# Writing out pair one of a Strassen-blocked projection by hand, and spreading the row factors with a split diagonal on TensorE

## The chip, the cores and the metric

The kernel runs on one core of one Trainium2 chip. The metric is the device time of one execution in microseconds; lower is better. All arithmetic is float32 in and out; the matrix products run on TensorE in its fp32r type, each operand split into a high and a low part and multiplied in three passes (high times low, low times high, high times high).

The engines are named as in the profile: PE is TensorE's matmul, PEld its weight load, DVE is VectorE, ACT is ScalarE, POOL is GpSimd and SP is SyncE, which issues nearly all transfers. Each engine runs its own instruction queue in order and waits on the others through semaphores.

## The reference, cut to what matters

One layer of a hybrid decoder trunk is applied to 1024 prompt rows and 32 sample rows, 1056 rows of 1024 channels in all. What the change touches is the norm ahead of the projection and the first groups of the projection's 24 column blocks:

```python
def _rmsnorm(x, g):
    xf = x.astype(jnp.float32)
    r = lax.rsqrt(jnp.mean(xf * xf, axis=-1, keepdims=True) + EPS)
    return (xf * r).astype(x.dtype) * g
...
    proj = jnp.einsum('bsd,de->bse', h, w_in)
    b_g, c_g, u, z_a, v, z_b = jnp.split(proj, ...)
    cu = c_g * u                      # then a 3-tap convolution along the rows
    y_a = b_g * yc * jax.nn.silu(z_a)
    # v: mean over a trailing window of 2, 4, 8 or 16 rows, minus the row, a 128x128 map
    y_b = pooled * pool_scale * jax.nn.silu(z_b)
    y = jnp.einsum('bse,ed->bsd', jnp.concatenate([y_a, y_b], axis=-1), w_out)
```

The output rows then get x added and a second norm.

## The kernel before, in words

The rows lie on the free axis: a tile is 128 channels by 1056 rows, cut into three column groups n0, n1, n2 of 352. The kernel does not scale x before the projection. It multiplies the weights by the norm's gain (`gain_w`, line 196), projects the unscaled x, and multiplies the results by the row factor r (`R`, the 1056 factors on every partition) or, for the product of c and u, by its square (`R2`).

The 24 column blocks are taken in twelve pairs (`PAIRS`, line 35). Pair 0 (v and z_b of group 0) is projected plainly while x arrives (`project_first`, line 180); its results stay unscaled in `vb` and `szb_0` (lines 499 and 526). From pair 1 on a pair is two blocks of 128 output channels, done over n0 and n1 by a Strassen scheme with eight block products of 12 matmuls (`block`, line 219), and plainly over n2 (`plain`, `plain1`: 24 matmuls for each side). The names: a block B11, B12, B21, B22 uses the weights as they are (tiles `wa` and `wb`), T1 to T4 use sums of weights (`tw`, made by `make_t`, line 202; split into `wc` and `wd`); S1 to S4 are sums of x made once. The accumulators in PSUM are a, b and c; `s1` is a copy of a after its first block, `t1` and `t2` are b plus `s1` after b's first and second block. `strassen` (line 388) writes one pair: PE order is B11 on a, T2 on b, T1 on c, left plain, B21 on a, T3 on b, right plain, T4 on b, B22 on c. T4 overwrites what `t2` reads, so PE's T4 waits for `t2` (line 439). The three hooks `early`, `middle` and `late` make the next pair's weights: load (1 MB, `load_w`), gain on ACT (8 instructions), sums on DVE, and four splits, each an ACT copy to fp32r (the high part) and a DVE subtraction (the low part), line 151 and 152.

The row factors: rows 0 to 639 are loaded once more row by row (`load_rows`, line 232) and squared on ACT with a sum along the row (`square_rows`, one instruction for each 128 rows, five in all). The other 416 rows are squared from the transposed x (`squares_head`, `squares_last`), summed over channels by DVE (`sums_last`) and over partitions by PE against a column of ones (`sums_rest`, line 265). `rows` (line 273) turns the 128 by 9 table of sums into factors with nine small instructions on DVE and ACT, writes the table to DRAM and reads it back broadcast to all partitions (lines 284 to 286).

What sets the order: inside the block from line 476, the engines PE, ACT, DVE and POOL run in program order, except that a scheduler may interleave this block with what comes after it; in the pairs from 2 on only PE is in program order, and the scheduler places the rest by its own priorities. Buffers are tiles of a pool under a tag; a new tile waits until the old one's readers are done. The tags that matter are `wt` (five buffers for split weights) and `wraw` (one buffer for a pair's raw weights, so that `load_w(p + 1)` waits for the last split of pair p).

Of the kernel before, what the change touches and what calls it, by code (L numbers as in the profile page):

```python
# [62 lines left out]
def trunk(ctx, tc, xt, xres, xct, w_first, w_in, w_out, pool_w, par, fg, sconv, spool,  # L63
# [194 lines left out]
    def sums_last(acc, sq):  # L258
        out = acc[:, REST:TC]
        vt(sq[0], sq[0], sq[1], op=ADD)  # L260
        vt(sq[0][:, :2], sq[0][:, :2], sq[2], op=ADD)
        vt(out, sq[0][:, 0], sq[0][:, 1], op=ADD)
        vt(out, out, sq[0][:, 2], op=ADD)

    def sums_rest(acc):
        pt = bank("rest")
        for t in range(NTT, NTOK):
# [3 lines left out]
            nc.scalar.copy(ss[:m, t:t + 1], pt[:m, i:i + 1])  # L271
# [116 lines left out]
    def strassen(p, S1, S2, S3, S4, hooks):  # L388
# [19 lines left out]
        if p == 1:  # L408
            a, s1, pL, pR = hooks["open"]
        else:  # L410
            a = bank(f"a_{p}")[:, :TN]
            s1 = snap(f"s1_{p}")
            block(a, p, "B11", A11, True, False)
            nc.scalar.copy(s1, a)
# [7 lines left out]
        if p > 1:  # L422
            block(c, p, "T1", S1, True, False)
        if p > 1:
            pL = plain(0, f"l_{p}")
        def scaled(n, pt):
            if p == 1:
                nc.scalar.copy(left[:, n], pt)
            else:
                vt(left[:, n], pt, scale[:, n], op=MUL)  # L430

        scaled(n2, pL)
# [19 lines left out]
        if p > 1:  # L452
            gt(left[:, n1], left[:, n1], scale[:, n1], op=MUL)
# [8 lines left out]
        elif q == "c":  # L462
            gt(up[:, 2:2 + 2 * TN], right[:, both], left[:, both], op=MUL)
# [12 lines left out]
    with tc.manual_schedule(engines={ET.PE, ET.Activation, ET.DVE, ET.Pool}):  # L476
# [38 lines left out]

        S1 = xtile("xa", "S1")
        split(S1, S1f)
        make_unit(1, "c")
        S3 = xtile("xb", "S3")
        split(S3, S3f)  # L520
        S2 = xtile("xc", "S2")
        split(S2, S2f)
        make_unit(1, "d")
        for n in (0, 1):
            for i in range(2):
                nc.scalar.copy(heads[i][:, cols[n]], pm[i, n])
# [4 lines left out]
        pL, pR = plain1(0), plain1(1)  # L531
        a1 = bank("a_1")[:, :TN]
        block(a1, 1, "B11", A11, True, False)
        s1 = snap("s1_1")
        nc.scalar.copy(s1, a1)  # L535
        block(a1, 1, "B21", A12, False, True)

        def early():
            gain_w(2)
            make_t(2)  # L540
            make_unit(2, "a")
            sums_last(acc, sq)

        def middle():
            make_unit(2, "d")
            make_unit(2, "c")
            xk.extend(load_rows(t) for t in range(2, NTT))
            for t in range(NTT):
                square_rows(t, xk[t])
# [256 lines left out]
```

## Time and profile before

| what | value |
|---|---|
| time, median of 3 runs (lowest to highest) | 411.41 us (411.21 to 414.06) |
| the profiled execution: its own time, its span | 411.48 us, 409.7 us |
| PE busy, share of the span | 369.8 us, 90% |
| DVE, ACT, POOL busy | 271.3 us (66%), 174.6 us (43%), 45.5 us (11%) |
| chain that ended last, by engine | PE 70%, DVE 11%, DMA 6%, ACT 6% |
| mean granted TensorE clock | 0.959 |

How to read it: times count from the span's start. A row of a timeline is start, duration, engine, line, operation, out<-in, shapes, and in brackets the idle time before it with what ended it. Two instructions that follow each other on one engine overlap by about 0.1 us in the records, so a row of instructions costs a little less than the sum of their durations; the chain of waits shows the durations without this overlap. A block of 12 matmuls takes 1.94 us there when the granted clock is full.

### The profile page before, as it was taken

How to read it: one execution, taken by the hardware profiler on the slowest of the kernel's cores; microseconds unless marked ns; L12 is line 12 of the kernel's file. 1: busy time of each engine (PE TensorE's matmuls, PEld its weight loads, DVE VectorE, ACT ScalarE, POOL GpSimd, SP SyncE). 2: the span in 40 equal slices, each digit the busy share in tenths (PEclk: the TensorE clock that was granted, in tenths of full speed). 3: DMA queues.
4: the chain of work that ended last, by engine and by line, in shares of the span. 5: the costliest groups of instructions: out<-in, count | busy, mean ns of one | idle time of the engine just before them, and what ended most of it. 6: DMA issues, size and time to landing. Idle time of an engine off the chain costs nothing.

```text
span 409.7 us, 5263 instructions
## 1 busy us (share of the span) xinstructions
PE 369.8 (90%) x2108; PEld 353.3 (86%) x2108; DVE 271.3 (66%) x387; ACT 174.6 (43%) x299; POOL 45.5 (11%) x28
## 2 busy tenths in 40 slices
PE   8999549930699999999999999999999999999993
PEld 5999539930699999999999999999998888999883
DVE  4888486229967878766779675688629926422493
ACT  5894954415252364526163545345107805111211
POOL 0000002005300303200300400020501000000000
PEclk9999887985699999999999999999999999999998
DMA  7932312110050204030020404140646970300042
GB/s 220 417 125 102 104 61 74 46 53 0 0 210 0 104 0 154 3 121 37 18 86 2 155 2 155 29 154 2 200 170 204 379 308 6 150 0 0 2 167 102
DMA packets 14680, 42.23 MB, mean 103 GB/s; under 512 B 4928, under 2 KB 6080, under 8 KB 13248
## 3 DMA queue, kind: packets, MB, share of 16 engines
q1 hardware_dynamic: 14512, 41.57, 28.2%
q8 instruction: 16, 0.26, 0.3%
q10 hardware_dynamic: 144, 0.33, 0.2%
q14 instruction: 8, 0.07, 0.1%
HBM read 33.46 MB, written 8.43 MB: 102 GB/s over the span
## 4 chain that ended last, share of the span: by engine, by line
PE 70%; DVE 11%; DMA 6%; ACT 6%; issue 2%; SPq 2%; POOL 1%; DVEq 0%; POOLq 0%; ACTq 0%
PE b L226 14%; PE po L636 13%; PE a L226 9%; PE pc L706 9%; PE c L226 9%; PE r L226 8%; PE l L226 8%; DMA rows<-mru 3%; DMA raw<-in_xt_dram 3%; DVE win L340 2%; PE pp L362 1%; ACT wraw L200 1%; SPq L106 1%; DMA R<-rows 1%; DVE tw L205 1%
## 5 line engine op out<-in xcount | busy, mean ns | idle before, releaser
L636 PE MATMUL po<-wo,mix 128*128 128x512 f32 (+1 forms) x264 | 56.7, 374 | 0.2 <-DVE mix L152 0.2
L636 PEld LDWEIGHTS po<-wo,mix 128*128 128x128 f32 x264 | 46.2, 188 | 10.2 <-DVE mix L152 0.8
L226 PE MATMUL a<-A,wa 128*128 128x352 f32 x264 | 47.9, 331 | 5.1 <-ACT s L535 5.1
L226 PE MATMUL b<-A,wd 128*128 128x352 f32 x132 | 26.8, 358 | 25.5 <-DVE t L439 25.4
L226 PEld LDWEIGHTS a<-A,wa 128*128 128x128 f32 x264 | 44.7, 194 | 5.4 <-ACT s L535 5.4
L226 PEld LDWEIGHTS b<-A,wd 128*128 128x128 f32 x132 | 24.6, 213 | 26.4 <-DVE t L439 26.4
L200 ACT ACTIVATE wraw<-wraw,gain 128x256 f32<-128x256 f32 x88 | 36.5, 499 | 12.9 <-DMA wraw<-in_w_in_dram 11.4
L226 PE MATMUL l<-pl,wa 128*128 128x352 f32 x240 | 40.4, 324 | 0.0
L226 PE MATMUL r<-pl,wb 128*128 128x352 f32 x240 | 40.4, 324 | 0.0
L226 PEld LDWEIGHTS l<-pl,wa 128*128 128x128 f32 x240 | 39.1, 188 | 0.0
L226 PEld LDWEIGHTS r<-pl,wb 128*128 128x128 f32 x240 | 39.1, 188 | 0.0
L706 PE MATMUL pc<-mix,wo 128*128 128x416 f32 x192 | 36.5, 351 | 0.0
L706 PEld LDWEIGHTS pc<-mix,wo 128*128 128x128 f32 x192 | 35.9, 188 | 0.6
L205 DVE TENSOR_TENSOR tw<-wraw 128x1024 f32<-128x1024 f32 x11 | 13.9, 1265 | 20.1 <-ACT wraw L200 20.1
L226 PE MATMUL b<-S,wc 128*128 128x352 f32 x132 | 23.2, 324 | 0.7 <-DVE t L421 0.7
L226 PE MATMUL c<-S,wb 128*128 128x352 f32 x132 | 23.8, 330 | 0.0
L226 PE MATMUL b<-S,wd 128*128 128x352 f32 x132 | 23.6, 325 | 0.0
L226 PE MATMUL c<-S,wc 128*128 128x352 f32 x132 | 23.4, 324 | 0.0
L151 ACT ACTIVATE wd<-tw 128x1024 fp32r<-128x1024 f32 x11 | 11.6, 1057 | 26.8 <-DVE tw L207 26.8
L226 PEld LDWEIGHTS c<-S,wb 128*128 128x128 f32 x132 | 22.4, 195 | 0.2 <-DVE y L440 0.2
L226 PEld LDWEIGHTS b<-S,wc 128*128 128x128 f32 x132 | 21.6, 188 | 1.0 <-DVE t L421 1.0
L226 PEld LDWEIGHTS b<-S,wd 128*128 128x128 f32 x132 | 21.7, 188 | 0.0
(178 smaller groups left out, 562.5 us busy)
## 6 DMA issues: line engine op xcount, KB each, us to landing
wraw<-in_w_in_dram SPq DMA_DIRECT2D x11, 1024.0 KB, 4.6
woraw<-in_w_out_dram SPq DMA_DIRECT2D x8, 512.0 KB, 6.3
raw<-in_xt_dram SPq DMA_DIRECT2D x4, 704.0 KB, 8.8
zt<-in_xres_dram SPq DMA_DIRECT2D x5, 512.0 KB, 6.7
spill_b<-yb SPq DMA_DIRECT2D x4, 528.0 KB, 4.1
mixraw<-spill_b SPq DMA_DIRECT2D x4, 528.0 KB, 6.8
out_yt_dram<-zt SPq DMA_DIRECT2D x4, 512.0 KB, 2.6
zc<-in_xct_dram SPq DMA_DIRECT2D x4, 416.0 KB, 6.6
```

Of the source, the lines that this page charges most:

```text
L106: nc.sync.dma_start(raw[n][:, k:k + m, :], xt[:, n * KD + k:n * KD + k + m, :])
L151: nc.scalar.activation(hi, src, AF.Copy)
L200: nc.scalar.activation(t, t, AF.Copy, scale=gain[:, k:k + 1])
L205: nc.vector.tensor_tensor(t[:, 0:2], w[:, 2:4], w[:, 0::2], op=ALU.subtract)
L226: nc.tensor.matmul(pt, t[:, a, i, k * P:(k + 1) * P], x[:, b, k], start=first and s == 0, stop=last and s == len(seq) - 1, skip_group_chec ...
L340: nc.vector.tensor_tensor(o[:, lo2:PM + SEQ], a[:, lo2:PM + SEQ], a[:, lo2 - s:PM + SEQ - s], op=ALU.add)
L362: nc.tensor.matmul(pt[:, :TN], pws[:, a, g, :], pooled[g][b][:, cols[n]], start=(s == 0), stop=(s == 2))
L636: nc.tensor.matmul(pt, mix[k][:, b, t * P:(t + 1) * P], wo[k][:, a, c], start=(k == 0 and s == 0), stop=(k == KD - 1 and s == 2))
L706: nc.tensor.matmul(pt, wo[k][:, a, d * P:(d + 1) * P], mix[k][:, b, T0:], start=(k == 0 and s == 0), stop=(k == KD - 1 and s == 2))
```

## The change: the diff, and how it moves instructions

Pair 1 no longer goes through `strassen`; its instructions are written out with the order of each engine, in the block that sets the order of PE, ACT, DVE and POOL. In it DVE makes the weight sums (`make_t(1)`) before the split of `wb`; ACT squares three of the five row tiles early, ahead of the four copies of pair 0's results, and takes the copy `s1` ahead of the two halves of S4; the row tiles lie in `R`, `R2`, `up` and one weight buffer (`x34`, tag `wt`) instead of `R`, `R2` and three tiles of the tag `tmp`. The four sums of `sums_rest` are copied out by two instructions instead of four.

The row factors take another way. `rows` splits the 128 by 9 table into a high part `rh` and a low part and multiplies a 128 by 128 identity (`ident`, made by POOL at the start) with each of the nine columns, which gives two tiles of 128 by 1056 (`dh` on ACT, `dl` on DVE) that are diagonal in each stretch of 128 columns. `rows_out`, called in pair 2 after its T1 block, multiplies them on PE with a 128 by 128 matrix of ones (6 matmuls of 352 columns), and ACT copies the result into `R` (three copies) and squares it into `R2`. The write to DRAM and the broadcast read are gone. What needs `R` (`scale_heads`: `after_u(0)`, `vb`, `szb_0`, `after_v(0)`, the pool weights) moved into pair 2's `early` hook. `pool_linear(0)` comes after pair 3 instead of pair 2, and in the pairs from 2 on POOL is in program order too.

```diff
+    ident = sm.tile([P, 19 * NB], F32, tag="swin", name="ident")[:, :P]
+    nc.gpsimd.memset(ident, 0.0)
+    nc.gpsimd.affine_select(out=ident, in_=ident, compare_op=ALU.not_equal, fill=1.0, base=0,
+                            pattern=[[-1, P]], channel_multiplier=1)
...
         vt(sq[0][:, :2], sq[0][:, :2], sq[2], op=ADD)
+        yield
         vt(out, sq[0][:, 0], sq[0][:, 1], op=ADD)
...
-            nc.scalar.copy(ss[:m, t:t + 1], pt[:m, i:i + 1])
+        nc.scalar.copy(ss[:, NTT:NTOK - 1], pt[:, :NTOK - 1 - NTT])
+        nc.scalar.copy(ss[:NSAMP, NTOK - 1:], pt[:NSAMP, NTOK - 1 - NTT:NTOK - NTT])
...
-        d = tc.dram_tile([NTOK * P], F32, name="rows")
-        nc.sync.dma_start(d.rearrange("(t p) -> p t", p=P), r)
-        nc.sync.dma_start(R, d[:TOK].partition_broadcast(P))
+        rh = sm.tile([P, NTOK], F32R, tag="rh", bufs=1, name="rh")
+        nc.scalar.activation(rh, r, AF.Copy)
+        vt(u, r, rh.bitcast(F32), op=ALU.subtract)
+        dh, dl = (tp.tile([P, TOK], F32R, tag="tmp", name=f"diag_{a}") for a in range(2))
+        for t in range(NTOK):
+            m = min(P, TOK - t * P)
+            nc.scalar.activation(dh[:, t * P:t * P + m], ident[:, :m], AF.Copy, scale=rh[:, t:t + 1].bitcast(F32))
+            nc.vector.tensor_scalar(dl[:, t * P:t * P + m], ident[:, :m], u[:, t:t + 1], None, op0=ALU.mult)
+        return dh, dl
+
+    def rows_out(diag):
+        for n in range(NT):
+            pt = bank(f"pr_{n}")[:, :TN]
+            for a in (1, 0):
+                nc.tensor.matmul(pt, onesr, diag[a][:, cols[n]], start=a == 1, stop=a == 0)
+            nc.scalar.copy(R[:, cols[n]], pt)
         nc.scalar.activation(R2, R, AF.Square)
...
+        block(c, p, "T1", S1, True, False)
+        if p == 2:
+            rows_out(diag)
+            gt(up[:, 2:], up[:, 2:], R2, op=MUL)
+        pL = plain(0, f"l_{p}")
...
-        xk = [load_rows(t) for t in range(2)]
+        xk = [load_rows(t, q[:, :D]) for t, q in enumerate((R, R2, up[:, 2:]))]
...
+        make_t(1)
         make_unit(1, "b")
+        load_w(2)
...
+        x34 = wp.tile([P, 2, D], F32, tag="wt", bufs=5, name="x34")
+        xk += [load_rows(t, x34[:, t - 3]) for t in (3, 4)]
+        for t in range(3):
+            square_rows(t, xk[t])
+        for n in (0, 1):
+            for i in range(2):
+                nc.scalar.copy(heads[i][:, cols[n]], pm[i, n])
+        S2 = xtile("xc", "S2")
+        split(S2, S2f)
+        make_unit(1, "d")
...
+        block(pa, 1, "B11", A11, True, False)
+        nc.scalar.copy(s1, pa)
+        block(pa, 1, "B21", A12, False, True)
         S4 = xtile("xd", "S4")
...
+        sums = sums_last(acc, sq)
+        next(sums)
+        nc.scalar.copy(t_0[:, n2], pL)
+        block(pc, 1, "T1", S1, True, False)
+        block(pb, 1, "T2", S2, True, False)
+        vt(t1, pb, s1, op=ADD)
+        gain_w(2)
+        nc.scalar.copy(t_0[:, n0], pa)
+        make_unit(2, "a")
+        block(pb, 1, "T3", S3, False, False)
+        vt(t2, pb, s1, op=ADD)
+        make_t(2)
+        vt(um[:, n1], pc, t2, op=ADD)
+        for t in (3, 4):
+            square_rows(t, xk[t])
+        make_unit(2, "d")
+        block(pb, 1, "T4", A22, False, True)
+        vt(t_0[:, n1], pb, s1, op=ADD)
+        block(pc, 1, "B22", S4, False, True)
+        vt(um[:, n0], pc, t1, op=ADD)
+        gt(up[:, 2:2 + 2 * TN], um[:, both], t_0[:, both], op=MUL)
+        vt(up[:, 2 + 2 * TN:], pR, t_0[:, n2], op=MUL)
+        for _ in sums:
+            pass
+        make_unit(2, "c")
+        sums_rest(acc)
+        diag = rows()
+        make_unit(2, "b")
...
+    def scale_heads():
+        after_u(0)
+        vt(vb[:, PM:], vb[:, PM:], R, op=MUL)
+        gt(szb[0], szb[0], R, op=MUL)
+        silu(szb[0])
+        pwraw = tmp("pwraw")[:, :NG * P].rearrange("p (g c) -> p g c", c=P)
+        nc.sync.dma_start(pwraw, pool_w)
+        split(pws, pwraw)
+        after_v(0)
...
-        with tc.manual_schedule(engines={ET.PE}):
+        with tc.manual_schedule(engines={ET.PE, ET.Pool}):
             strassen(p, S1, S2, S3, S4, {"early": early, "middle": middle, "late": late})
-            if p == 2:
+            if p == 3:
                 pool_linear(0)
```

Three places show how instructions move. The rows name line, operation, out<-in and size; numbers behind names are buffers.

ACT, in pair 1, up to the copy `s1` (last row). `vb` and `szb` copies are pair 0's results, `S` are the high parts of S3 (raw_88), S2 (raw_89) and S4 (S4f). Before:

```order
L151 ACTIVATE wc_391<-tw_382 128x1024
L151 ACTIVATE S_394<-raw_88 128x1408
L151 ACTIVATE S_397<-raw_89 128x1408
L151 ACTIVATE wd_400<-tw_382 128x1024
L526 COPY vb<-pm_0_240 128x352
L526 COPY szb_140<-pm_0_241 128x352
L526 COPY vb<-pm_1_298 128x352
L526 COPY szb_140<-pm_1_299 128x352
L151 ACTIVATE S_407<-S4f_378 128x704
L151 ACTIVATE S_407<-S4f_379 128x704
L535 COPY s_1_475<-a_462 128x352
```

Now:

```order
L155 ACTIVATE wc_397<-tw_381 128x1024
L155 ACTIVATE S_400<-raw_88 128x1408
L241 ACTIVATE R,ss<-R 128x1024
L241 ACTIVATE R_134,ss<-R_134 128x1024
L241 ACTIVATE up,ss<-up 128x1024
L524 COPY vb<-pm_0_246 128x352
L524 COPY szb_145<-pm_0_247 128x352
L524 COPY vb<-pm_1_304 128x352
L524 COPY szb_145<-pm_1_305 128x352
L155 ACTIVATE S_413<-raw_89 128x1408
L155 ACTIVATE wd_416<-tw_381 128x1024
L542 COPY s_1_474<-a_471 128x352
```

Three squares and the four copies now stand between the high parts of S3 and S2, and `s1` follows the split of `wd` directly; the two halves of S4 come behind it.

DVE, in pair 2, up to `t2` (last row), behind the scaling of `vb` by `R` and the convolution. `win`, `pl` and `first` are the pooling of group 0, `pws` the pool weights, `tw` and `wa` pair 3's weights, `z` pair 2's left side. Before:

```order
L207 TENSOR_TENSOR tw_746<-wraw_736,tw_746 128x512
L340 TENSOR_TENSOR win_0_648<-vb 128x1038
L379 SCALAR_TENSOR_TENSOR yc_638<-up,part,yc_638 128x1024
L381 SCALAR_TENSOR_TENSOR yc_638<-scb,part,yc_638 128x32
L379 SCALAR_TENSOR_TENSOR yc_638<-up,part,yc_638 128x1024
L381 SCALAR_TENSOR_TENSOR yc_638<-scb,part,yc_638 128x32
L345 SCALAR_TENSOR_TENSOR pl_652<-win_0_648,vb 128x1024
L347 SCALAR_TENSOR_TENSOR pl_652<-swin_0_649,spb 128x32
L351 TENSOR_TENSOR first_655<-win_0_648,part 128x1
L152 TENSOR_TENSOR wa_750<-wraw_736,wa_750 128x1024
L352 TENSOR_TENSOR pl_652<-first_655,vb 128x1
L439 TENSOR_TENSOR t_2_778<-b_682,s_2_668 128x352
```

Now:

```order
L156 TENSOR_TENSOR pws<-pwraw,pws 128x512
L364 SCALAR_TENSOR_TENSOR pl_757<-win_0_753,vb 128x1024
L366 SCALAR_TENSOR_TENSOR pl_757<-swin_0_754,spb 128x32
L370 TENSOR_TENSOR first_760<-win_0_753,part 128x1
L209 TENSOR_TENSOR tw_777<-wraw_767 128x1024
L371 TENSOR_TENSOR pl_757<-first_760,vb 128x1
L156 TENSOR_TENSOR wa_781<-wraw_767,wa_781 128x1024
L210 TENSOR_TENSOR tw_777<-wraw_767,tw_777 128x512
L444 TENSOR_TENSOR z_649<-a_651,R 128x352
L211 TENSOR_TENSOR tw_777<-wraw_767,tw_777 128x512
L156 TENSOR_TENSOR pooled_1_764<-pl_757,pooled_0_763 128x1056
L447 TENSOR_TENSOR t_2_809<-b_666,s_2_652 128x352
```

Between the window and `t2` there now stand also the split of `pws`, all three sums of `tw` (before, one of them lay ahead of `R`), a scaling of `z` (a second one stands just ahead of the window) and the split of `pooled`.

PE, at the end of pair 2: `l`, `r` are the plain sides, `a`, `b`, `c` the accumulators (pair 2: a_667, b_682, c_683 before and a_651, b_666, c_681 now). Before:

```order
L226 MATMUL r_781<-pl_136,wb_599 128x352 x12
L226 MATMUL b_682<-A_133,wd_556 128x352 x12
L226 MATMUL c_683<-S_407,wb_599 128x352 x12
L362 MATMUL pp_0_849<-pooled_1_659,pws 128x352
L362 MATMUL pp_0_849<-pooled_0_658,pws 128x352 x2
```

Now:

```order
L230 MATMUL r_812<-pl_141,wb_641 128x352 x12
L230 MATMUL a_885<-A_136,wa_781 128x352 x12
L230 MATMUL b_900<-S_413,wd_838 128x352
L230 MATMUL b_666<-A_138,wd_567 128x352 x12
L230 MATMUL c_681<-S_502,wb_641 128x352 x12
L230 MATMUL b_900<-S_413,wd_838 128x352 x11
```

Pair 3's first block (`a_885`) and the first matmul of its second (`b_900`) now stand ahead of pair 2's T4 (`b_666<-A_138`), and the nine matmuls of `pool_linear(0)` are gone from here.

More of the change, by code (lines that the diff above doesn't have):

```diff
@@ L406, in plain @@
             return pt
[L408 to L414, printed above, removed]
+        a = bank(f"a_{p}")[:, :TN]
+        s1 = snap(f"s1_{p}")
+        block(a, p, "B11", A11, True, False)
+        nc.scalar.copy(s1, a)
         b = bank(f"b_{p}")[:, :TN]
-        c = bank(f"c_{p}")[:, :TN]
-        if p == 1:
-            block(c, p, "T1", S1, True, False)
         block(b, p, "T2", S2, True, False)
@@ L421, in strassen @@
         vt(t1, b, s1, op=ADD)
[L422 to L432, printed above, removed]
+        c = bank(f"c_{p}")[:, :TN]
+        block(c, p, "T1", S1, True, False)
[3 more added lines that the diff above has]
+        pL = plain(0, f"l_{p}")
+        vt(left[:, n2], pL, scale[:, n2], op=MUL)
         hooks["early"]()
-        if p > 1:
-            block(a, p, "B21", A12, False, True)
-        scaled(n0, a)
+        block(a, p, "B21", A12, False, True)
+        vt(left[:, n0], a, scale[:, n0], op=MUL)
         block(b, p, "T3", S3, False, False)
@@ L440, in strassen @@
         vt(right[:, n1], c, t2, op=ADD)
-        if p > 1:
-            pR = plain(1, f"r_{p}")
+        pR = plain(1, f"r_{p}")
         if q == "v":
@@ L451, in strassen @@
         vt(left[:, n1], b, s1, op=ADD)
-        if p > 1:
-            gt(left[:, n1], left[:, n1], scale[:, n1], op=MUL)
+        gt(left[:, n1], left[:, n1], scale[:, n1], op=MUL)
         block(c, p, "B22", S4, False, True)
@@ L505, in trunk @@
             vt(S4f[h], raw[0][:, KH + 2 * h:KH + 2 * h + 2], S2f[:, 2 * h:2 * h + 2], op=ALU.subtract)
-        make_t(1)
-        load_w(2)
+        S1 = xtile("xa", "S1")
+        split(S1, S1f)
+        make_unit(1, "c")
+        S3 = xtile("xb", "S3")
+        split(S3, S3f)
+        x34 = wp.tile([P, 2, D], F32, tag="wt", bufs=5, name="x34")
[8 more added lines that the diff above has]
+        make_unit(1, "d")
+        t_0, um = tmp("t_0"), tmp("um_0")
         def plain1(i):
@@ L513, in plain1 @@
             return pt
[L516 to L526, printed above, removed]
+        pL, pR = plain1(0), plain1(1)
+        pa, pb, pc = (bank(f"{q}_1")[:, :TN] for q in "abc")
+        s1, t1, t2 = (snap(f"{q}_1") for q in ("s1", "t1", "t2"))
+        block(pa, 1, "B11", A11, True, False)
+        nc.scalar.copy(s1, pa)
+        block(pa, 1, "B21", A12, False, True)
         S4 = xtile("xd", "S4")
@@ L530, in trunk @@
             split2(S4[:, 0, ks], S4[:, 1, ks], S4f[h])
[L531 to L549, printed above, removed]
@@ L551, in late @@
-        def late():
-            make_unit(2, "b")
-        strassen(1, S1, S2, S3, S4, {"early": early, "middle": middle, "late": late, "open": (a1, s1, pL, pR)})
+        sums = sums_last(acc, sq)
[8 more added lines that the diff above has]
+        block(pb, 1, "T3", S3, False, False)
@@ L555, in trunk @@
+        make_unit(2, "c")
         sums_rest(acc)
-        rows()
-        gt(up[:, 2:], up[:, 2:], R2, op=MUL)
-        gt(szb[0], szb[0], R, op=MUL)
-    vt(vb[:, PM:], vb[:, PM:], R, op=MUL)
+        diag = rows()
+        make_unit(2, "b")
     nc.sync.dma_start(scb[:, :, 0:2 * NB], sconv)
     nc.sync.dma_start(spb[:, :, 0:15 * NB], spool)
-    pwraw = tmp("pwraw")[:, :NG * P].rearrange("p (g c) -> p g c", c=P)
-    nc.sync.dma_start(pwraw, pool_w)
-    split(pws, pwraw)
-    after_u(0)
-    after_v(0)
@@ L567, in trunk @@
-    silu(szb[0])
+    def scale_heads():
[7 more added lines that the diff above has]
+        after_v(0)
     for p in range(2, NP):
@@ L572, in early @@
         def early():
+            if p == 2:
+                scale_heads()
             if nxt:
```

10 lines of the change are left out of this document (4 added, 6 removed).

## The prediction, made before the changed kernel was run

> **What bounds the kernel now.** I read the page's slices first, then the waits, then the chain of waits in order of time, and last DVE's, ACT's and POOL's timelines of the stretch that these point to.
>
> ```profile
> span 409.7 us, 5263 instructions
> PE   8999549930699999999999999999999999999993
> ```
>
> PE is the bound from about 106 us to the end: nothing but nines. It has three gaps, in the slices at 41, 51 and 82 to 106 us. The waits name what ended them:
>
> ```profile
> PE b L226 <- DVE t L439: 25.4, 2, 20.3
> DVE vb L559 <- DMA R<-rows: 11.8, 1, 11.8
> ```
>
> The chain in order of time shows both sides of each gap:
>
> ```profile
> 44.96 0.35 ACT s L535
> 45.36 3.65 PE a L226 x12
> ...
> 74.01 12.21 DMA rows<-mru
> 86.23 3.82 DMA R<-rows
> ...
> 105.46 0.45 DVE t L439
> 105.95 3.89 PE b L226 x12
> ...
> 117.28 1.94 PE c L226 x12
> ```
>
> At 45.36 PE had waited for the copy `s1`. At 105.95 it had waited 20.3 us for `t2` of pair 2, a 0.45 us addition that stood on DVE behind everything that needs `R`; `R` left for DRAM at 74.01 and was back at 90.05, and the additions behind it took until 105.91, 15.9 us after. Twelve matmuls take 1.94 us in the row at 117.28 and 3.65 and 3.89 us after the gaps: a long wait is paid for again with a slow restart of 1.7 to 1.95 us.
>
> One more thing in DVE's queue decides a later step:
>
> ```profile
> 91.30 2.55 POOL L557 TENSOR_TENSOR up<-up,R 128x1056 f32<-128x1056 f32 x1 [20.86 <-ACT R L287]
> 91.85 2.16 DVE L342 TENSOR_TENSOR swin<-spb 128x144 f32<-128x144 f32 x1
> 93.81 2.48 POOL L558 TENSOR_TENSOR szb<-szb,R 128x1056 f32<-128x1056 f32 x1
> 93.94 2.90 DVE L207 TENSOR_TENSOR tw<-wraw,tw 128x512 f32<-128x512 f32 x1
> 100.78 3.36 POOL L383 TENSOR_TENSOR yc<-yc,R 128x1056 f32<-128x1056 f32 x1 [4.49 <-DVE yc L381]
> 101.76 2.42 DVE L347 SCALAR_TENSOR_TENSOR pl<-swin,spb 128x32 f32<-128x32 f32 x1
> 158.05 1.56 DVE L364 SCALAR_TENSOR_TENSOR yb<-pp,part,szb 128x352 f32<-128x352 f32 x3
> 158.59 1.72 POOL L463 TENSOR_TENSOR up<-um,t 128x704 f32<-128x704 f32 x1
> ```
>
> A DVE instruction with two SBUF operands that meets a running POOL instruction ends only after it: 144 elements took 2.16 us, 32 elements 2.42 us. Of the 15.9 us about 6.4 are such blocking. With one operand in PSUM (L364) DVE runs on at 0.52 us each.
>
> **Part one: pair 1, up to pair 2's first matmul.**
>
> ```profile
> 30.21 1.23 DVE L152 TENSOR_TENSOR wb<-wraw,wb 128x1024 fp32r<-128x1024 f32 x1 [1.53 <-ACT wb L151]
> 38.14 2.10 PE L226 MATMUL a<-A,wa 128*128 128x352 f32 x12
> 39.87 1.38 ACT L151 ACTIVATE S<-raw 128x1408 fp32r<-128x1408 f32 x1 [3.33 <-DVE S L152]
> 43.47 1.50 ACT L151 ACTIVATE S<-S4f 128x704 fp32r<-128x704 f32 x2
> 53.44 1.22 DVE tw L205
> 56.10 1.13 DVE wa L152
> 58.05 1.04 ACT L238 ACTIVATE R<-R 128x1024 f32<-128x1024 f32 x1
> 59.37 0.54 DVE acc L262
> 67.16 2.19 PE L226 MATMUL a<-A,wa 128*128 128x352 f32 x12
> 67.90 2.54 POOL L463 TENSOR_TENSOR up<-um,t 128x704 f32<-128x704 f32 x1 [67.46 <-DVE um L455]
> 68.80 2.20 DVE L152 TENSOR_TENSOR pws<-pwraw,pws 128x512 fp32r<-128x512 f32 x1
> ```
>
> The weight sums (2.6 us, from 53.44 to 56.10) fill the 1.53 us in which DVE waited for `wb`, so S3's low part ends 1.5 us earlier and ACT can start S2's high part at 38.3 instead of 39.87. The three early squares (1.04 each) and the four copies (1.4) fit in the 3.33 us that ACT waited there and the copies' old place: free; without that gap they would cost 1.2. S2 and `wd` take 2.3, `s1` follows at 40.5 instead of behind copies and S4, and PE goes on at 41.0 instead of 45.36, after 0.8 us of waiting, so without the slow restart (1.7). Then, in PE's order: three blocks to 46.9; `t1`, T3 from 47.7; `t2`, now behind `wa`'s split, T4 from 50.5; the sums of `tw` (2.6) and `um` stand ahead of B22, which runs from 53.5 to 55.5. Now the loss: POOL's product starts 0.2 us after `um` n0 (56.2) and holds DVE's last two additions of `acc` (0.54 each), which have two SBUF operands, until POOL ends: 1.65 us as the pair 67.90/68.80 shows (POOL ran from DVE's end at 68.80 to 70.44). `acc` is done at 59.1; PE, whose four `rest` matmuls stand ahead of pair 2, waits 3.6 us and starts pair 2 at 59.5 instead of 67.16.
>
> Is that wait long enough for a slow restart? Granted clock (third number from the right) in three 0.3 us windows:
>
> ```profile
> 44.90:45.20 0.30, 0.00 (x0) 0.00 (x0) 0.30 (x2) 0.30 (x3) 0.00 (x0) 0.95 0.00 0
> 58.60:58.90 0.30, 0.00 (x0) 0.00 (x0) 0.30 (x1) 0.30 (x1) 0.00 (x0) 0.87 0.00 0
> 89.30:89.60 0.30, 0.00 (x0) 0.00 (x0) 0.00 (x0) 0.00 (x0) 0.00 (x0) 0.91 0.11 42
> ```
>
> The clock fell at about 45.2, 58.9 and 89.6 us, that is 4.9, 3.1 and 3.9 us after the last matmul had ended. So 3.6 us is survived in two of three; I take no slow restart, and 1.8 us as the rival. [...]
>
> **Part two: from there to `R`.**
>
> ```profile
> 72.44 0.17 DVE L277 TENSOR_SCALAR mru<-ss 128x9 f32<-128x9 f32 x1 [1.45 <-ACT ss L271]
> 73.81 0.17 DVE L283 TENSOR_TENSOR mru<-mru 128x9 f32<-128x9 f32 x1
> L200 ACT ACTIVATE wraw<-wraw,gain 128x256 f32<-128x256 f32 x88 | 36.5, 499 | 12.9 <-DMA wraw<-in_w_in_dram 11.4 <-DVE yc L379 1.0 <-DVE A L152 0.6
> L377 ACT ACTIVATE yc<-scb,part 128x32 f32<-128x32 f32 x4 | 1.3, 318 | 0.0
> ```
>
> Sums copied by 60.0; `wc`'s split holds DVE until 60.2; the nine-wide chain takes 1.5 (72.44 to 73.98), r at 61.7. On ACT the copy `s1` of pair 2 stands ahead of `rh` and waits for PE's block (59.5 + 1.94), so `rh` ends at 62.2. The diagonals are not in the trace. On ACT 128 elements lie between 32 (0.318) and 256 (0.499): nine cost 2.9 to 4.5, and I take 0.35 each, 3.1, to 65.3. On DVE the nearest rows are 0.17 (nine wide) and 0.54 (352 wide): 1.5 to 4.9, taken as 2.3, beside ACT's. PE reaches the six matmuls after T2 and T1 at 65.3 (59.5 + 3 x 1.94), so they wait for nothing and cost 6 x 0.16 = 1.0. `wb`'s split on ACT (1.0) lies ahead of the copies; three of these at 0.35 give `R` at 67.3 instead of 90.05. The ends: ACT's and DVE's upper prices put it 1.4 and 2.0 later; the lower ones change nothing, since PE's T1 ends last. The identity costs nothing, since POOL is idle until 67.90 (its row), nor do the row loads, needed only at 33 and 48 us.
>
> **Part three: `R` to pair 2's T4.** The 15.9 us stay (the same three POOL instructions block DVE), and ahead of `t2` come now `pws` (0.6), one more sum of `tw` (1.2), two scalings of z (0.45 each) and the split of `pooled` (1.2): 3.9, together with the slightly later start of POOL (one copy and square more) 20.0. So `t2` ends at 67.3 + 20.0 = 87.3. PE after its six matmuls does left, B21, T3 and right (six blocks' worth, 11.6) until 77.9, then waits for `wa` of pair 3, whose low part stands 3.3 us ahead of `t2`'s end: 84.0. After 6 us of waiting the restart is slow: the block takes 3.65, the one matmul 0.2, and T4 starts at 87.9, just behind `t2`. Weights are no bound:
>
> ```profile
> wraw<-in_w_in_dram SPq DMA_DIRECT2D x11, 1024.0 KB, 4.6
> ```
>
> `load_w(3)` waits for `wb`'s split, 67.2, lands at 72, and its eight gains are done at 76, while DVE asks for them at 82; a landing 6 us later would begin to cost.
>
> **The sum.** T4, B22 and eleven matmuls of T2 (1.94 + 1.94 + 1.8) bring pair 3's T1 to 93.6. Before it started at 117.28, with the nine matmuls of `pool_linear(0)` (1.45) behind it, which are still to come now. The gain is 117.3 - 93.6 - 1.45 = 22.2; behind it PE's work is the same. The profiled execution took 411.48 (span 409.7 and 1.8 around it), as the median of the runs, 411.41. **Forecast: 389.3 us.**
>
> **Rivals.**
>
> - *Slow restart at the `rest` matmuls*: all behind is 1.8 later, since pair 2's first block delays `s1` and with it `rh`: 391.1. For it: one fall of the clock after 3.1 us. Against it: two after 3.9 and 4.9.
> - *POOL blocks DVE less than counted*, because the queues meet otherwise: up to 6.4 less, then PE waits for nothing at 77.9 and keeps its clock: about 382.5. Against it: three blocked instructions out of three.
> - *Part is handed back* in pairs 3 and 4, where DVE carries the deep pooling and the next load comes 4 us later against PE than before: two waits of some 2 us, 393.5.
> - *Slower*: pair 3's `wa` and first T2 matmul now stand on PE ahead of pair 2's T4, so its 1 MB load is on PE's path. Beyond 6 us of lateness each microsecond counts; it must land 28 us late (after 33 instead of 4.6) to be slower than before: at 35 us, 413.5. Nothing in the trace took longer than 12.21.
>
> **How the numbers follow.** Chances: forecast 0.60, slow restart 0.22, less blocking 0.08, handed back 0.07, slower 0.01, and 0.02 for gains that vanish otherwise (near 411). A measurement here tells about 1% from no change, 4 us. Faster by more than that: 0.97; within: 0.02; slower: 0.01. The range of the likeliest case is 387.5 to 391.5 (diagonals 2.0 later, POOL a little less); with the slow restart and part of the handed-back case above, and half of the way to less blocking below, it is 385 to 395.
>
> **What would show it.** Right: no transfer of the table; `s1` of pair 1 near 40.5; `acc`'s addition stretched to about 2 us by POOL near 57; `R` at 66 to 69; a PE wait of about 6 us for `wa` near 78, with half clock behind it; no new PE wait over 1 us behind 95. Wrong: `R` later than 72, a PE wait behind 95, or a PE block of 12 in 3.6 us or more near 60 (the first rival).

## The result and the profile after

The changed kernel takes 394.34 us in the median of four executions (391.62, 393.04, 395.64, 396.48), the kernel before 411.35 us on the same chip: a ratio of 0.957, 95% interval 0.949 to 0.965. The profiled execution is the one of 391.62 us. In the changed kernel's rows the helpers stand 4 lines lower than before (the splits' low parts are L156, the block matmuls L230); further down the lines differ more.

The page of the changed kernel, its span and PE in 40 slices:

```profile
span 389.6 us, 5300 instructions
PE   8999859949999999999999999999999999999993
```

Of the three gaps two are left: the first, near 41, has shrunk to an 8; the 5 is the slice of 49 to 58 us, and of the long gap one slice remains, the 4 at 78 to 88. The waits of PE name both (total, times, longest):

```profile
PE a L230 <- DVE wa L156: 5.4, 1, 5.4
PE rest L274 <- DVE acc L267: 3.4, 1, 3.4
```

PE's timeline through both gaps (start, time from first to last, what it waited for ahead of it):

```profile
41.19 2.20 PE L230 MATMUL a<-A,wa 128*128 128x352 f32 x12 [0.73 <-ACT s L542]
...
53.72 2.21 PE L230 MATMUL c<-S,wb 128*128 128x352 f32 x12 [0.82 <-DVE um L560]
59.32 0.98 PE L274 MATMUL rest<-one,acc 128*128 128x1 f32 x8 [3.39 <-DVE acc L267]
60.24 3.50 PE L230 MATMUL a<-A,wa 128*128 128x352 f32 x12
...
85.94 3.60 PE L230 MATMUL a<-A,wa 128*128 128x352 f32 x11 [5.40 <-DVE wa L156]
...
89.63 2.83 PE L230 MATMUL b<-A,wd 128*128 128x352 f32 x12
...
96.02 2.11 PE L230 MATMUL c<-S,wc 128*128 128x352 f32 x12
```

Twelve matmuls fill 2.1 to 2.2 us at full clock; the block at 60.24, right behind the wait of 3.39 us, took 3.50, with a granted clock of 0.50 from 60.6 to 63.9. That is the slow restart that the forecast left out. The second restart, at 85.94, lasted longer than the forecast had it: T4's block took 2.83 instead of 2.1. The engines behind the two waits, each from its own timeline; DVE and POOL near 57 us:

```profile
56.85 1.85 DVE L266 TENSOR_TENSOR acc<-sq 128x352 f32<-128x352 f32 x1
58.74 0.52 DVE L267 TENSOR_TENSOR acc<-acc,sq 128x352 f32<-128x352 f32 x1
```

```profile
56.66 1.67 POOL L568 TENSOR_TENSOR up<-um,t 128x704 f32<-128x704 f32 x1 [55.35 <-DVE um L567]
```

The same addition over 352 elements takes 0.52 us in the second row and 1.85 in the first, which ends at 58.70, just after POOL's product (58.33). ACT's path to `R`, and DVE's to `t2`:

```profile
40.70 0.43 ACT L542 COPY s<-a 128x352 f32<-128x352 f32 x1
63.77 0.45 ACT L430 COPY s<-a 128x352 f32<-128x352 f32 x1 [2.78 <-PE a L230]
64.12 0.21 ACT L291 ACTIVATE rh<-mru 128x9 fp32r<-128x9 f32 x1
64.43 2.66 ACT L296 ACTIVATE diag<-ident,rh 128x128 fp32r<-128x128 f32 x9
68.14 1.17 ACT L305 COPY R<-pr 128x352 f32<-128x352 f32 x3
```

```profile
61.89 0.17 DVE L288 TENSOR_TENSOR mru<-mru 128x9 f32<-128x9 f32 x1
64.64 1.81 DVE L297 TENSOR_SCALAR diag<-ident,mru 128x128 fp32r<-128x128 f32 x9
78.73 2.49 DVE L366 SCALAR_TENSOR_TENSOR pl<-swin,spb 128x32 f32<-128x32 f32 x1
81.14 2.41 DVE L370 TENSOR_TENSOR first<-win,part 128x1 f32<-128x1 f32 x1
88.61 0.51 DVE L447 TENSOR_TENSOR t<-b,s 128x352 f32<-128x352 f32 x1
```

Set against the steps of the prediction (us from the start of the span; ends worked out as start and duration of the rows above):

| step | predicted | measured |
|---|---|---|
| `s1` of pair 1 starts; PE goes on | 40.5; 41.0 | 40.70; 41.19 |
| T3, T4, B22 of pair 1 start | 47.7, 50.5, 53.5 | 47.89, 50.70, 53.72 |
| `acc` done; PE's wait for it | 59.1; 3.6 | 59.26; 3.39 |
| pair 2 starts | 59.5 | 60.24 |
| r done; `rh` done | 61.7; 62.2 | 62.06; 64.33 |
| nine diagonals on ACT; on DVE | 3.1; 2.3 | 2.66; 1.81 |
| `R` done | 67.3 | 69.31 |
| `R` to the end of `t2` | 20.0 | 19.81 |
| PE's wait for `wa` of pair 3 | 6 | 5.40 |
| pair 3's T1 starts | 93.6 | 96.02 |

Behind that T1 the two kernels differ by less than 0.5 us: 117.28 - 96.02 - 1.45 is 19.8, and 411.48 - 19.8 is 391.7, where the profiled execution has 391.62. From this T1 to the end of the span it is also 293.6 us in the traces of e0_again, e1_acc_first, e4_s1_behind, e5_pe_kept_busy, e6_products_on_dve and e8_squares_late below, so what sets these apart lies ahead of it.

### The profile page after: what moved, and what is told of

Its sections match the earlier page's. It is cut to its first block, busy times and chain, and to the rows that moved or that the text cites. A ratio compares the mean times of both kernels' runs of the same rounds, so it can differ in the third digit from the quotient of the medians.

```text
span 389.6 us, 5300 instructions
## 1 busy us (share of the span) xinstructions
PE 369.6 (95%) x2114; PEld 353.5 (91%) x2114; DVE 273.0 (70%) x397; ACT 177.2 (45%) x310; POOL 43.2 (11%) x30
## 5 line engine op out<-in xcount | busy, mean ns | idle before, releaser
L230 PE MATMUL a<-A,wa 128*128 128x352 f32 x264 | 49.6, 338 | 6.1 <-DVE wa L156 5.4
L230 PEld LDWEIGHTS a<-A,wa 128*128 128x128 f32 x264 | 45.7, 198 | 6.7 <-DVE wa L156 5.7
L230 PE MATMUL l<-pl,wa 128*128 128x352 f32 x240 | 40.4, 324 | 0.0
L230 PE MATMUL r<-pl,wb 128*128 128x352 f32 x240 | 40.4, 324 | 0.0
L230 PEld LDWEIGHTS l<-pl,wa 128*128 128x128 f32 x240 | 39.1, 188 | 0.0
L230 PEld LDWEIGHTS r<-pl,wb 128*128 128x128 f32 x240 | 39.1, 188 | 0.0
L230 PE MATMUL b<-A,wd 128*128 128x352 f32 x132 | 24.0, 331 | 0.6 <-DVE t L558 0.6
L230 PE MATMUL c<-S,wb 128*128 128x352 f32 x132 | 23.2, 324 | 0.8 <-DVE um L560 0.8
L230 PE MATMUL b<-S,wc 128*128 128x352 f32 x132 | 23.2, 324 | 0.6 <-DVE t L553 0.6
L230 PE MATMUL b<-S,wd 128*128 128x352 f32 x132 | 23.7, 327 | 0.0
L230 PEld LDWEIGHTS b<-A,wd 128*128 128x128 f32 x132 | 22.5, 195 | 0.9 <-DVE t L558 0.9
L230 PE MATMUL c<-S,wc 128*128 128x352 f32 x132 | 23.1, 324 | 0.0
L230 PEld LDWEIGHTS c<-S,wb 128*128 128x128 f32 x132 | 21.6, 188 | 1.1 <-DVE um L560 1.1
L230 PEld LDWEIGHTS b<-S,wc 128*128 128x128 f32 x132 | 21.6, 188 | 0.9 <-DVE t L553 0.9
L230 PEld LDWEIGHTS b<-S,wd 128*128 128x128 f32 x132 | 22.2, 191 | 0.0
```

Source lines behind the costliest of these rows:

```text
L230: nc.tensor.matmul(pt, t[:, a, i, k * P:(k + 1) * P], x[:, b, k], start=first and s == 0, stop=last and s == len(seq) - 1, skip_group_chec ...
```

## The experiments

The theory: the 20 us between the two profiled executions are made of an earlier end of pair 1 and of the row factors' way without DRAM; 5 us of what the order could give are lost at the `rest` matmuls, since POOL's product blocks DVE's addition and PE's clock falls around that wait; and what is left behind `R` is DVE's work with POOL's blocking in it. The rivals are named in each expectation. Three groups shared a chip within each group: the first four kernels (before: 412.39 us), the next four (412.01) and the last (412.69).

| run | median us (lowest to highest, executions) | ratio to before, 95% interval |
|---|---|---|
| e0_again | 393.51 (391.21 to 394.49, 6) | 0.9538 (0.9513 to 0.9562) |
| e1_acc_first | 388.12 (387.43 to 388.79, 4) | 0.9412 (0.9392 to 0.9433) |
| e2_rows_dram | 404.00 (403.19 to 404.61, 4) | 0.9796 (0.9776 to 0.9817) |
| e4_s1_behind | 396.90 (393.53 to 398.48, 4) | 0.9598 (0.9562 to 0.9634) |
| e5_pe_kept_busy | 390.28 (389.53 to 393.15, 6) | 0.9479 (0.9452 to 0.9507) |
| e6_products_on_dve | 385.78 (384.59 to 386.52, 4) | 0.9365 (0.9337 to 0.9392) |
| e7_pooling_late | 387.91 (387.59 to 388.34, 4) | 0.9420 (0.9396 to 0.9443) |
| e8_squares_late | 387.68 (387.12 to 387.86, 4) | 0.9411 (0.9388 to 0.9435) |
| e9_both | 384.30 (382.11 to 387.51, 4) | 0.9321 (0.9249 to 0.9393) |

### e0_again: the changed kernel, unchanged

> The changed kernel, unchanged, for the spread of its times. If the 391.6 to 396.5 us of its first four executions come from the chip (a clock that opens later or lower at one of the gaps), the executions of one kernel will again lie some 4 us apart while the kernel before repeats within 0.5 us, and the profile will show the same order of waits with another granted clock: PE's wait of 3.4 us for `rest` near 59, half clock behind it, a wait of about 5.4 us for pair 3's wa. Rival: it was a chance of that chip; then the executions agree within 1 us, near 391.6.

Six executions lie 3.3 us apart; the kernel before lay within 2.0 us in eleven, not within 0.5. The profile repeats the first one (a wait of 3.40 us for `rest`, then a block of 3.56). So the spread belongs to the kernel and not to one chip, and the expectation that before repeats much better was too strong.

### e1_acc_first: `acc` ahead of POOL's product

```
         sums = sums_last(acc, sq)
-        next(sums)
+        for _ in sums:
+            pass
...
         vt(up[:, 2 + 2 * TN:], pR, t_0[:, n2], op=MUL)
-        for _ in sums:
-            pass
         make_unit(2, "c")
```

> The last two additions of acc stand with the first ones, ahead of POOL's product. Theory (POOL's product blocks DVE's addition, and PE's `rest` matmuls wait for that): the 3.4 us wait at `rest` is gone, no half clock near 60, pair 2 starts near 56.5 instead of 60.2 and R comes near 64.5 to 66 instead of 69.3; the profiled time falls by 3.5 to 5.5 us, to 386 to 388. Rival one (R's path is set by ACT's and DVE's other work, weight splits and diagonals, and not by rest): R stays within 1 us and so does the time. Rival two (the freed time meets a later load): R comes earlier, but PE's wait for wa of pair 3 grows from 5.4 to 9 us and the time stays.

5.4 us less than e0_again in the median. The theory spoke of the profiled execution, which is 3.8 less (387.43 against 391.21), at the lower end of its 3.5 to 5.5; the rest may be spread, which is 1.4 us here against 3.3 in e0_again. PE's timeline of this kernel at the place, DVE's, and ACT's copies of `R`:

```profile
55.41 0.88 PE L274 MATMUL rest<-one,acc 128*128 128x1 f32 x8
56.22 2.20 PE L230 MATMUL a<-A,wa 128*128 128x352 f32 x12
...
82.11 3.60 PE L230 MATMUL a<-A,wa 128*128 128x352 f32 x11 [6.07 <-DVE wa L156]
```

```profile
56.51 2.59 DVE L156 TENSOR_TENSOR wc<-tw,wc 128x1024 fp32r<-128x1024 f32 x1
```

```profile
64.35 1.12 ACT L305 COPY R<-pr 128x352 f32<-128x352 f32 x3
```

The wait and the half clock are gone, pair 2 starts 4.0 us earlier, and both rivals fall: `R` is done at 65.47 instead of 69.31, and PE's wait for `wa` grew by 0.7, not by 3.6. POOL's product still blocks DVE, but now the split of `wc` (2.59 us instead of 1.22), for which PE does not wait. What a blocked instruction costs is the wait behind it.

### e2_rows_dram: the row factors through DRAM again

```
-        rh = sm.tile([P, NTOK], F32R, tag="rh", bufs=1, name="rh")
...
-        return dh, dl
+        d = tc.dram_tile([NTOK * P], F32, name="rows")
+        nc.sync.dma_start(d.rearrange("(t p) -> p t", p=P), r)
+        nc.sync.dma_start(R, d[:TOK].partition_broadcast(P))
...
-            nc.scalar.copy(R[:, cols[n]], pt)
```

> The row factors go through DRAM again (table written, read by a broadcast), with pair one's new order and the early squares kept; rh, the diagonals and the six matmuls are left out. Theory: r is ready near 62 to 63, write and broadcast take 12.2 us and a few tenths, the two transfers' issue and R2 add some 3 us, so R comes near 76 to 78 instead of 69.3, t2 of pair 2 as much later, and the time is 7 to 9 us longer: 399 to 401. So the split diagonal is worth 8 of the 20 us and the order of pair one the rest. Rival: the wait for R is hidden by other work of pair 2 or the DVE chain behind R, so less than 3 us longer.

10.5 us more than e0_again, more than the 7 to 9 expected; the rival falls. DVE's row at which `R` arrives, and the DMA issues from 55 to 85 us (KB each, us from issue to landing):

```profile
82.40 0.53 DVE L430 TENSOR_TENSOR z<-l,R 128x352 f32<-128x352 f32 x1 [14.73 <-DMA R<-rows]
```

```profile
wraw<-in_w_in_dram SPq DMA_DIRECT2D x1, 1024.0 KB, 15.7
R<-rows SPq DMA_DIRECT2D x1, 528.0 KB, 6.5
...
rows<-mru SPq DMA_DIRECT2D x1, 4.5 KB, 13.0
```

The two transfers took 13.0 and 6.5 us, where the kernel before had 12.21 and 3.82: the expectation used the old durations. SP issued the table's write at 62.81 and the next weight load at 63.95; that load took 15.7 us instead of 4.8 in the kernel before, and the broadcast, issued at 75.80, ran beside its end. Of the 18.9 us that e0_again gains on its chip (412.39 - 393.51), the diagonals are 10.5 against this slower way through DRAM, and everything else in the diff is 8.4. Of that rest only `s1` and the squares are undone by themselves below; no run undoes the earlier weight sums, the later `pool_linear(0)` or POOL's program order alone.

### e4_s1_behind: `s1` behind S4's high part on ACT

```
-        block(pa, 1, "B11", A11, True, False)
-        nc.scalar.copy(s1, pa)
-        block(pa, 1, "B21", A12, False, True)
         S4 = xtile("xd", "S4")
         for h in range(2):
             ks = slice(2 * h, 2 * h + 2)
             split2(S4[:, 0, ks], S4[:, 1, ks], S4f[h])
+        block(pa, 1, "B11", A11, True, False)
+        nc.scalar.copy(s1, pa)
+        block(pa, 1, "B21", A12, False, True)
```

> On ACT, s1 of pair one stands behind both halves of S4's high part again (PE's B11/B21 are issued behind S4's split in the same order among themselves; PE's own order is unchanged). Theory (PE waits for s1 before B21): s1 at about 42.2 instead of 40.7, PE's second block starts 1.5 to 2.2 us later, at 42.7 to 43.4, with 2.2 to 3 us of waiting and full clock behind; all behind it as much later, so the time rises by 1.5 to 2.2 us, or by up to 4 if the clock falls in that wait. Rival (T4's or B22's operands set pair one's end, not PE): under 0.5 us.

3.4 us more than e0_again in the median, between the theory's 2.2 and 4. Its profiled execution (398.48), the slowest of the four, shows the case with the fallen clock:

```profile
44.31 3.89 PE L230 MATMUL a<-A,wa 128*128 128x352 f32 x12 [2.97 <-ACT s L546]
47.99 3.10 PE L230 MATMUL c<-S,wc 128*128 128x352 f32 x12
```

The second block starts 3.1 us later than in the changed kernel, of which 0.9 stand already ahead of pair 1 (its first block starts at 39.23 instead of 38.35), and two blocks at half clock add 2.7. So PE's waits in pair 1 do set the end of the pair, and the early `s1` is one of the terms that carry the gain.

### e5_pe_kept_busy: idle matmuls in the wait for `rest`

```
         pt = bank("rest")
+        for _ in range(18):
+            nc.tensor.matmul(pt[:, 64:64 + TN], onesr, pl[0][:, 0, 0], start=True, stop=True)
```

> The changed kernel with 18 idle matmuls (one tile of x, into unused columns of the bank of `rest`; their result is read by nobody) between B22 of pair one and the `rest` matmuls, so that PE works for 2.9 of the 3.4 us in which it waits for acc; all else as in the changed kernel. Theory (the restart at half clock after that wait is a cost of its own, 1.5 to 2.8 us by execution, and its chance is what spreads the times): pair 2 still starts near 59.8, but its first block takes 2.1 to 2.2 us instead of 3.5; the time is 1.5 to 3 us lower, near 391, and its executions lie within 2 us. Rival (the spread comes from the first 15 us, where the loads land, or from the wait for wa at 80 us): the spread stays at 3 us or more, and the time falls by less than 1.5.

390.28 us, 3.2 less than e0_again (2.4 less by the two ratios to before, 0.0059 of 412). With its wait filled PE has full clock behind it:

```profile
62.70 0.98 PE L276 MATMUL rest<-one,acc 128*128 128x1 f32 x8 [0.54 <-DVE acc L267]
63.61 2.21 PE L230 MATMUL a<-A,wa 128*128 128x352 f32 x12
```

So the restart is a cost of its own and most of the theory holds. Its last part does not: four executions lie at 389.5 to 390.3 and two at 392.3 and 393.15, 3.6 us in all. The profiled one is that of 393.15, and it shows where its 3 to 4 us went. ACT and PE:

```profile
23.51 3.31 ACT L204 ACTIVATE wraw<-wraw,gain 128x256 f32<-128x256 f32 x8 [2.30 <-DMA wraw<-in_w_in_dram]
```

```profile
42.99 2.64 PE L230 MATMUL a<-A,wa 128*128 128x352 f32 x12 [2.41 <-ACT s L544]
45.43 3.23 PE L230 MATMUL c<-S,wc 128*128 128x352 f32 x12
```

ACT started on pair 1's weights 1.8 us later than in the changed kernel, since their load landed later (there ACT waits 0.60 us at this place, and not for the load). `s1` came as much later, PE waited 2.41 us instead of 0.73, and 1.5 us behind that wait, at 44.5, the clock fell: another 1.6 us in two blocks. The rival's place, the first loads, has its share in the spread.

### e6_products_on_dve: POOL's three products behind `R` made by DVE

```
-            gt(up[:, 2:], up[:, 2:], R2, op=MUL)
+            vt(up[:, 2:], up[:, 2:], R2, op=MUL)
...
-        nc.gpsimd.tensor_tensor(yc, yc, R, op=ALU.mult)
+        (nc.vector if j == 0 else nc.gpsimd).tensor_tensor(yc, yc, R, op=ALU.mult)
...
-        gt(szb[0], szb[0], R, op=MUL)
+        vt(szb[0], szb[0], R, op=MUL)
```

> acc first as in e1_acc_first, and the three products that POOL makes behind R for pair 2 (up with R2, yc with R, szb with R) made by DVE. Theory (POOL's products stretch DVE's small additions from some 0.2 to 1.8, 2.5 and 2.4 us, and that chain is what PE's wait for wa ends with): the three short ones fall to 0.3 or less, together 6.0 us less, the three products cost DVE 3 x 1.25 = 3.75, so PE's wait for wa falls from 6.1 to about 3.9 and the time by 2 us against e1_acc_first, to 386. Rival one (the short ones are long for another reason): they stay, the wait grows by 3.75, 391.5. Rival two (ACT's silu or gains end last there): no change, 388.

385.78 us, 2.3 less than e1_acc_first (1.9 by the two ratios to before), as the theory had it. The three small instructions on DVE, each beside no product of POOL now:

```profile
75.60 0.30 DVE L361 TENSOR_TENSOR swin<-spb 128x144 f32<-128x144 f32 x1
...
76.96 0.19 DVE L366 SCALAR_TENSOR_TENSOR pl<-swin,spb 128x32 f32<-128x32 f32 x1
77.06 0.15 DVE L370 TENSOR_TENSOR first<-win,part 128x1 f32<-128x1 f32 x1
```

2.49 and 2.41 us became 0.19 and 0.15. PE's wait for `wa` fell from 6.07 to 3.2, but in two pieces, 1.30 for its high part on ACT (the silu now stands ahead of the gains) and 1.86 for the low part.

### e7_pooling_late: the pooling behind pair 2's last block

```
         after_u(0)
-        vt(vb[:, PM:], vb[:, PM:], R, op=MUL)
+
+    def scale_v():
+        vt(vb[:, PM:], vb[:, PM:], R, op=MUL)
...
         def late():
+            if p == 2:
+                scale_v()
```

> acc first as in e1_acc_first, and the scaling of vb and szb with the pooling behind them (eleven instructions of DVE, one of POOL, silu) moved behind pair 2's last block; the convolution on up stays. Theory (DVE's work between R and t2 is what PE waits 6.1 us for): t2 of pair 2 and wa of pair 3 are ready within some 10 us of R, PE's wait and the half clock behind it (some 2 us) are gone, and the time falls by 6 to 8 us to 380 to 382. Rival (the same DVE work is late in pair 3 instead, ahead of wa or t2 of pair 4 or of the first pooled product): PE waits there, and the time falls by less than 3 us, 385 to 388.

387.91 us: the rival. The wait of 6.07 us is gone and pair 3's T1 starts at 87.02 instead of 91.78, but the gain is handed back in two pieces on PE:

```profile
82.18 0.42 PE L230 MATMUL b<-S,wd 128*128 128x352 f32 x1 [0.54 <-ACT wd L155]
83.79 3.43 PE L230 MATMUL b<-S,wd 128*128 128x352 f32 x11 [1.19 <-DVE wd L156]
...
126.89 2.68 PE L230 MATMUL b<-A,wd 128*128 128x352 f32 x12 [2.60 <-DVE t L447]
```

What made `t2` of pair 4 late in the third row is not shown. A product of POOL (szb, 2.71 us from 108.71) stretches a row of DVE in pair 3, the first one here; but e9_both has the same stretch, the second row, and no wait in pair 4.

```profile
109.77 2.75 DVE L359 TENSOR_TENSOR win<-vb 128x1038 f32<-128x1038 f32 x1
```

```profile
108.69 2.74 DVE L359 TENSOR_TENSOR win<-vb 128x1038 f32<-128x1038 f32 x1 [0.41 <-POOL vb L459]
```

One difference between the two is on ACT: in e7_pooling_late its silu waits for POOL's other szb product, the split of `wb` stands behind the silu, and pair 4's load, which needs that split, is issued at 91.44. In e9_both it is issued at 88.71, though all there stands 1.8 us later.

```profile
88.12 1.09 ACT L330 ACTIVATE szb<-szb 128x1056 f32<-128x1056 f32 x1 [3.74 <-POOL szb L584]
```

### e8_squares_late: the early squares put back

```
-        for t in range(3):
-            square_rows(t, xk[t])
...
-        for t in (3, 4):
+        for t in range(5):
             square_rows(t, xk[t])
```

> acc first as in e1_acc_first, and the three early row squares put back on ACT beside the other two, behind wa of pair 2. Theory (both places are hidden: early they lie in a wait of ACT for S3's low part, late in one for the sums of tw): no change within 0.7 us of e1_acc_first, s1 up to 0.2 us earlier. Rival (the early place was worth something): three squares of 1.04 us delay wd of pair 2 on ACT and with it PE's second block of pair 2 or the copies of the sums; 1 to 3 us longer, 389 to 391.

387.68 against 388.12: no change, as the theory had it. The hole that the squares had filled is open again on ACT, and `s1` starts at 40.69, as in the changed kernel:

```profile
38.46 1.38 ACT L155 ACTIVATE S<-raw 128x1408 fp32r<-128x1408 f32 x1 [3.20 <-DVE S L156]
```

### e9_both: e6 and e7 together

> acc first, the three products behind R on DVE as in e6_products_on_dve, and the pooling moved behind pair 2's last block as in e7_pooling_late. Theory (pair 2's wait is DVE's work between R and t2, and e7 gave its 4 us back in pairs 3 and 4 because POOL's products still stretched DVE's instructions there): with t2 near 75 PE does not wait at all before pair 3's second operand wd, waits 1 to 3 us there, and pair 4's wait of 2.6 us for t2 is gone: 382 to 384. Rival (DVE's whole work from R to pair 4 is the bound, wherever it stands): the waits move again and the time stays at e6's 385.8 or above.

384.30 us, just above the theory's 382 to 384; its four executions reach from 382.11 to 387.51, though, so that it can't be told from e6_products_on_dve and the rival is not excluded. Pair 4's wait is gone as expected; PE's timeline shows what is left:

```profile
85.03 0.43 PE L230 MATMUL b<-S,wd 128*128 128x352 f32 x1 [1.58 <-ACT wd L155]
86.29 3.32 PE L230 MATMUL b<-S,wd 128*128 128x352 f32 x11 [0.83 <-DVE wd L156]
```

The profiled execution also had half clock from 11.5 to 15 us, among the first loads (24 matmuls at 11.45 took 5.67 us, 4.14 in the changed kernel), so all its later times stand 1.8 us behind.

Every run with `acc` first is faster than both kernels, and so is e5_pe_kept_busy; the lowest are e6_products_on_dve and e9_both, 0.937 and 0.932 of the kernel before.

## Why the prediction was right and where it was wrong

**Right: the chain, step by step.** The table above follows it to 0.2 us through pair 1, and to 0.2 us from `R` to `t2`. The runs bear out the reasons too: the early `s1` (e4_s1_behind, 3.4 us when undone), the free squares (e8_squares_late, nothing when undone), POOL's blocking of `acc` as the cause of the wait at `rest` (e1_acc_first), and the blocking of small additions as part of the way to `t2` (e6_products_on_dve). There the total is right and one of its parts is another: three instructions were blocked as forecast, but one of them is `first` (2.41 us), and the sum of `tw` that was blocked in the kernel before runs free. The runs show that blocking at one instruction: 2.49 us beside POOL in the changed kernel and 0.19 without in e6_products_on_dve, for the same 32 elements.

**Wrong: "3.6 us is survived in two of three; I take no slow restart".** With this wait the restart was slow in the changed kernel, e0_again and e4_s1_behind: the blocks behind it took 3.50, 3.56 and 3.89 us. The sign that the prediction named for it, a block of 3.6 us or more near 60, was just missed by the changed kernel (3.50). The step failed in its reading. It took the time from the last matmul to the fall of the clock as what a wait must exceed. The granted clock (third number from the right) around the fall in the changed kernel shows something else:

```profile
57.09:60.50 3.41, 1.18 (x9) 1.15 (x10) 3.28 (x3) 0.16 (x2) 1.24 (x1) 0.95 0.00 0
60.50:61.00 0.50, 0.50 (x4) 0.50 (x4) 0.17 (x1) 0.26 (x3) 0.00 (x0) 0.52 0.00 0
```

The clock fell at 60.5, when PE had been at work again for 1.2 us. In the 3.41 us up to the fall (the step of the clock's changes in the last section) PE had worked 1.18. (This trace reads 0.95 where the others read 1.00; the blocks take the same 2.1 us.) In these traces a fall goes with the share of work in such a stretch, and not with a pause of a certain length: the falls listed in the last section have between 0 and 1.75 us of work in the 3.4 us ahead of them. By this the restart was to be expected: wherever such stretches of 3.4 us begin, a wait of 3.4 us covers at least half of one and leaves it 1.7 us of work or less, an estimate from these figures. The kernel before had shown it: its fall at 58.8 came 3.1 us after the last matmul, with 0.36 us of work in the 3.4 us ahead of it.

**Mis-sized: the `rest` matmuls.** They were counted as four in the 0.4 us from `acc` to pair 2's start; they are eight instructions in 0.98 us, so pair 2 starts 0.7 us late (0.16 of it is `acc` itself). With the slow block that makes `s1` of pair 2, and `rh` behind it on ACT, 2.1 us late, and `R` 2.0: ACT's and DVE's diagonals were 0.4 and 0.5 us cheaper than taken, which changes nothing, since PE's three blocks end last there, as the prediction had it. The second restart was mis-sized too: half clock (granted 0.50) lasted two stretches, from 84.4 to 91.2, and T4's block with it, so that from T4 to T1 it is 6.4 us instead of 5.7. Together that is the first rival with its mechanism, and its 391.1 is 0.5 us short of the profiled execution's 391.62.

**Not foreseen: the executions spread.** The median lies 2.7 us above the profiled execution, which is the fastest of its four. The median of 394.34 lies in the stated range only by the range's upper end: the likeliest case ended at 391.5, the slow restart makes that 393.3, and what lies above was put there for work handed back in pairs 3 and 4. No trace of the changed kernel shows that; from pair 3's T1 on the time is the same in the execution of e4_s1_behind that took 398.48 us as in those of 391 us. That the range holds the median is luck as far as this part goes. Where the spread comes from is shown for other kernels only: a late load and the fall behind it in e5_pe_kept_busy, half clock among the first loads in e9_both. For the changed kernel it stays open: no trace of one of its longer executions exists, and its mean clock does not order them (0.980 with 396.48 us and 0.981 with 393.04; in e0_again 0.985 twice, 3.3 us apart). The other rivals did not come in its two traces: nothing was handed back, and no load was late on PE's path.

## What to carry to other kernels

Before pricing a wait on PE, look at the 3.4 us around it: in these traces the clock fell to half behind stretches with 1.75 us of work or less, with one exception (1.68 in e2_rows_dram, last section). Moving two additions of 0.5 us ahead of a POOL product was worth 5.4 us here. When an engine is blocked, ask which of its instructions is waited for, and let the blocking fall on another. Work moved behind a wait must still fit before the next one: eleven instructions moved out of pair 2 (e7_pooling_late) closed a wait of 6 us and opened others, with half clock behind them, of the same worth.
